# Two transformer blocks on one core: twelve more tiles by seven products, a convolution moved beside them, and a modulation taken in steps

## The chip, the cores and the metric

One core of one Trainium2 chip. The metric is the device time of one execution in microseconds; the kernel before has a median of 2616.32 us over 3 runs (2611.67 to 2616.39). The profile is of a run of its own, which took 2621.87 us.

## What is computed

Two blocks over 1024 tokens of width 1024, all in float32. The first block has a modulated norm, an SSM branch with a GLU, an attention over selected keys, a merge and an FFN. The second block, on which most of the change falls, projects its normed input `h` to gates and branch inputs and has three branches:

```python
gate_pre, a_in, a_z, b_uv, b_z, q, k, v, c_z, f_pre = split_columns(h @ w_in)

mod = cond @ w_mod + b_mod                       # first block: shift, scale, gate
u = rms_norm(h, norm1_g) * (1 + scale1) + shift1

# second block, branch a (conformer): a convolution of 31 taps over the tokens
a = a_in[..., :512] * sigmoid(a_in[..., 512:])
a = causal_depthwise_conv(a, conv_w, conv_b)
y_a = (silu(layernorm(a)) * silu(a_z)) @ w_a
# branch b (gmlp): v is mixed over the tokens of a chunk
y_b = (u * mixed(rmsnorm(v)) * silu(b_z)) @ w_b
# branch c (fox): attention with a forget gate
y_c = (attention(rmsnorm(q), rmsnorm(k), v, f_pre) * silu(c_z)) @ w_c
x = x + (g_a * y_a + g_b * y_b + g_c * y_c) @ w_out
```

## The kernel before

**Numbers.** Every float32 product on TensorE is made of three, each operand split in a high and a low part (`mm3`): high by high, high by low, low by high. ScalarE casts the high part (`wh`, L130), VectorE or GpSimd subtracts it for the low part (`wl`, L122). So a tile of 128 output columns over all tokens and a depth of 1024 takes 8 depth steps x 2 halves of 512 tokens x 3 products = 48 matmuls in `linear`. `linear_t` gives token-major output: 48 matmuls of 256 columns for a pair of token tiles.

**Seven products.** `wino` computes a pair of 128-column tiles by Strassen's scheme in Winograd's form: both the pair of tiles and the two halves of the tokens are cut in two along the depth too, and 7 products of quarter size take the place of 8. `wino_weights` makes sums of weights (`s<-wq`, GpSimd) and splits them (`vh`, `vl`). A pair costs 7 products x 4 depth steps x 3 = 84 matmuls of 512 columns where `linear` takes 96; in exchange the products must be added up: they are held as `snap` and reach the eviction function either whole or as a part to which a second one (`more`) is added.

**Order.** The program is recorded as one list for each engine by a scheduler; the engines run their lists in order and wait for each other by semaphores. The code steers the order with generators: `aside` is advanced once after each tile of `linear` (L159 matmuls), and in `wino` by a rate (`together`), so that VectorE work is spread beside TensorE work. `self.pace` and `self.tick` tie loads and other instructions to a matmul so that they are not put earlier.

**Stages that the change touches, in the order of TensorE:**

- The start, 0 to 80 us: transposes of `norm1`, then the first modulation. `mod_fast(part, half)` makes 512 values of scale or shift: 8 matmuls `p<-wmod` of one row by 256 columns (the other 256 columns are summed by VectorE into `macc`), a copy of the row to `macc` by ScalarE, 4 `turn` matmuls that turn it to a column, and an addition. `rest(half)` makes scale, scales 4 pages `xnt` on ScalarE, makes shift, and writes the split input `uh`, `ul` for half of the depth. The first two tiles of `proj1` come as 48 matmuls over the first half of the depth, then `between()`, which is all of `rest(1)`, then 48 over the second half.
- `glu`, about 490 to 583 us: 16 tiles of 24 matmuls `pl<-yh,wh`, with the key selection of the first attention (`topk`) on VectorE beside them as `aside`; GpSimd makes `wl` here. The `aside` step that ends `topk` runs straight on into `attend`, whose first act is a unit of logits (`pl<-akh,aqq`, then an exponent with a sum at L1182).
- `conv_in` 1541 to 1628 us; `plain_gates` to 1715 us: 8 tiles of `linear` for `a_z` (columns 4096, to DRAM page `az`) and `c_z` (columns 7680, to `fd`).
- `gates2` 1715 to 1943 us: 12 pairs by seven products, with `conv(0)` and `conv(1)` beside them, all of whose 31 taps are VectorE instructions of 512 tokens into PSUM (`p<-ca,small,p`).
- `fox` 1943 to 2124 us: q, k and v by `linear_t`, each tile with its norm (`xsl`), and a return through DRAM as `xraw`, scaled by GpSimd and transposed by TensorE. Beside it `conformer` runs `conv(2)` and `conv(3)` with every second tap on ScalarE (`ct`) and GpSimd (`cy<-cy,ct`), then the layer norm: a sum of squares `sqa` reduced by TensorE, a small chain on VectorE, and `diag` matrices by ScalarE from which TensorE spreads the factors; twice, for the mean and for the variance.
- `gmlp` 2124 to 2210 us: v by `linear_t`, then for each of 4 groups one tile of `b_z`, one of `b_u` by `linear`, and the mixing matmuls `p<-wst,gv`, whose result VectorE multiplies with both.

Of the kernel before, what the change touches and what calls it, by code (L numbers as in the profile page):

```python
# [12 lines left out]
AF = mybir.ActivationFunctionType  # L13
OP = mybir.AluOpType
# [3 lines left out]
T = 1024  # L18
# [50 lines left out]
class Core:  # L69
# [118 lines left out]
    def linear(self, w, cols, kt, xh, xl, evict, r0=0, half=None, between=None):  # L188
# [287 lines left out]
    def mod_fast(self, part, half):  # L476

        p = self.p1()
        acc = self.pg("macc2", bufs=2)
        for k in range(0, 8, 2):  # L480
# [4 lines left out]
            for j in range(2):  # L485
                c = self.cond[:, k + j:k + j + 1]
                self.mm(p[0:1, :256], c, w[:, j, 0:256], k + j == 0, k + j == 7)
# [4 lines left out]
        self.act(acc[0:1, 0:256], p[0:1, :256])  # L492
        p = self.p1()
        for j in range(4):
            n = 1 if j < 2 else 128
            self.mm(p[:, j:j + 1], acc[:n, j * 128:(j + 1) * 128], self.ones[:n, 0:1])
        m = self.small([4])
        c0 = part * 8 + half * 4
        self.tt(m, p[:, 0:4], self.v["b_mod"][:, c0:c0 + 4], OP.add)
        return m  # L500
# [40 lines left out]
    def norm1(self):  # L541
# [22 lines left out]
        def rest(half):  # L564

            ks = range(4 * half, 4 * half + 4)
            gs = self.small([4])
            self.stt(gs, self.mod_fast(1, half), 1.0, self.v["norm1_g"][:, 4 * half:4 * half + 4], OP.add, OP.mult)
            for k in ks:
                self.act(xnt[:, k], xnt[:, k], scale=gs[:, k % 4:k % 4 + 1])  # L570
            shift = self.mod_fast(0, half)
            self.wmark = self.last_mod
# [9 lines left out]
        rest(0)  # L582
        return uh, ul, lambda: rest(1)
# [1018 lines left out]
    def keep_x2(self):  # L1602
# [3 lines left out]
        for k in range(8):  # L1606
            x = self.pg("h", bufs=8)
            self.load(x, self.hd2[k], self.pace)
            self.ts(x, x, fg[:, k:k + 1])
            o = blocks(self.pg("xc", bufs=2))  # L1610
# [9 lines left out]
    def fox(self, hh, hl):  # L1620
# [74 lines left out]
        for j, (c0, gain) in enumerate(((6656, self.v["k_norm_g_2"]), (6144, gq))):  # L1695
            for g in range(2):
# [30 lines left out]
                start(unit_norm(g, j, gain, x, ss))  # L1727
        for g in range(2):
# [11 lines left out]
            self.linear_t(self.wraw(w, 0, 8, 7168 + 256 * g, 256), 8, hh, hl, ev_v)  # L1740

    def plain_gates(self, hh, hl, norm):
# [4 lines left out]
        def ev(dst, scale):  # L1747
            def f(m, p):
                z = self.pg("gst", bufs=2)
                self.mark = self.act(z, p, AF.Tanh, scale=0.5)  # L1750
                self.stt(z, z, 1.0, p, OP.add, OP.mult)
                if scale != 1.0:
                    self.act(z, z, scale=scale)
                self.load(dst(m), z)
# [11 lines left out]
    def gates2(self, x4, first):  # L1766

# [3 lines left out]
        for pair in range(12):  # L1771
# [11 lines left out]
            jobs.append((lambda pair=pair: self.wino_weights(w, 256 * pair), ev))  # L1783
        self.wino(jobs, x4, first)
# [113 lines left out]
    def gmlp(self, hh, hl):  # L1898
# [5 lines left out]
        for g in range(2):  # L1904
            def ev_v(i, p):
                x = v[i][:, :, 256 * g:256 * g + 256]
# [6 lines left out]
        def mix(t):  # L1913
            if t == 0:
                self.tt(ss[:, 0], ss[:, 0], ss[:, 1], OP.add)
                r = self.rsqrt_cols(ss[:, 0], 512)
                for i in range(8):
                    x = v[i // 2][:, i % 2]
                    self.act(x, x, scale=r[:, i:i + 1])
            yield  # L1920
            mx = self.pg("bb", bufs=4)
            for s in range(2):
                q = blocks(self.p1())
                for i in range(4):
                    self.mm(q[:, i], v[2 * s + i // 2][:, i % 2, t * 128:(t + 1) * 128], wst[:, t * 128:(t + 1) * 128])
                self.stt(blocks(mx[:, 512 * s:512 * s + 512]), q, self.v["gmlp_norm_g_2"][:, t:t + 1],
                         wst[:, None, 512 + 128 * t:640 + 128 * t].to_broadcast([128, 4, 128]), OP.mult, OP.add)
            self.bb.append(mx)
            yield
        steps = (None for t in range(4) for _ in mix(t))  # L1930
        self.hold = []

        def ev_z(m, p):
            th = self.pg("gz", bufs=2)
            self.act(th, p, AF.Tanh, scale=0.5)
            self.stt(th, th, 1.0, p, OP.add, OP.mult)
            self.hold.append(th)
            next(steps)

        def ev_u(m, p):  # L1940
            th = self.hold.pop(0)
            self.tt(th, th, p, OP.mult)
            next(steps)
            t = len(self.bb) - 1
            self.tt(self.bb[t], self.bb[t], th, OP.mult)
            self.show(f"bb{t}", self.bb[t])
        for t in range(4):
            self.linear(w, [(5632 + 128 * t, 128)], 8, hh, hl, ev_z)
            self.linear(w, [(4608 + 128 * t, 128)], 8, hh, hl, ev_u)

    def conv_in(self, hh, hl, norm):
# [3 lines left out]
        self.cyd = self.dram([2, 128, T], "cyd")  # L1955
# [24 lines left out]
    def conv(self, t, both):  # L1980


        gp, cw = self.nc.gpsimd, self.cw
# [3 lines left out]
        taps = range(30, -1, -2 if both else -1)  # L1987
        odd = list(range(29, -1, -2)) if both else []
        if both:
            y2 = self.pg("cy", bufs=2)  # L1990
            self.later(gp.memset(y2[:, 0:1], 0.0), self.pace)
        for h in range(2):
            acc = self.p1()
            c0 = 512 * h
            for n, k in enumerate(taps):
# [7 lines left out]
                if n % 2 == 1 and odd:  # L2003
                    for k2 in odd[:2]:
                        s, wk = 30 - k2, cw[:, k2, t:t + 1]
                        if s == 1:
                            i = self.act(y2[:, 1:], at[:, :T - 1], scale=wk)
                        else:
                            z = self.pg("ct", bufs=2)
                            i = self.act(z[:, s:], at[:, :T - s], scale=wk)  # L2010
                            self.tt(y2[:, s:], y2[:, s:], z[:, s:], OP.add, gp)
                        self.later(i, self.pace)
                    odd = odd[2:]
                if n % (4 if both else 8) == (3 if both else 7) and n < len(taps) - 1:
                    yield
            if h == 0 or not both:
                self.act(y[:, c0:c0 + 512], acc)
            else:
                self.tt(y[:, 512:], acc, y2[:, 512:], OP.add)
# [186 lines left out]
```

## Time and profile before

| | |
|---|---|
| median of 3 runs | 2616.32 us |
| profiled run | 2621.87 us, span 2620.2 us |
| mean granted TensorE clock | 0.984 |
| TensorE matmuls busy | 2515.9 us (96%) |
| VectorE / ScalarE / GpSimd busy | 63% / 43% / 32% |
| TensorE instructions of matmul | 12849 |

The profiled run is longer than the shown runs' median by 5.6 us. A busy time of TensorE counts overlapping rows once: a matmul of 512 columns has a row of 0.39 us, and the next one starts 0.23 us after it, so 96% says that TensorE was hardly ever without a matmul, not how fast each went. In 2620.2 us there are 104 us in which TensorE was idle.

### The profile page before, as it was taken

The page shows a single profiled execution, that of the slowest core. Times are in us where ns is not written, and L with a number is a line of the kernel's source. Part 1 is how long each engine was busy: PE and PEld are TensorE (multiplying, and loading weights), DVE is VectorE, ACT ScalarE, POOL GpSimd, SP SyncE. Part 2 cuts the span into 40 slices and gives each one's busy share as a digit, 9 for nine tenths or more (in the row PEclk, how much of TensorE's full clock was granted, in tenths as well). Part 3 has the DMA queues.
Part 4 walks back from the last instruction along what each step waited for, and adds up shares of the span by engine and source line. Part 5 has one row for each costly group of instructions (what it writes and reads, how often), then busy time and mean ns, then how long its engine had stood idle before and what let it go on. Part 6 is the DMA issues. An engine that isn't in the chain of part 4 may idle for free. (4 is left out here: it accounts for less than half of the span.)

```text
span 2620.2 us, 35143 instructions
## 1 busy us (share of the span) xinstructions
PE 2515.9 (96%) x12849; PEld 2119.9 (81%) x12849; DVE 1653.9 (63%) x2882; ACT 1129.7 (43%) x2144; POOL 847.9 (32%) x889
## 2 busy tenths in 40 slices
PE   6998999979999999999999999999999999999999
PEld 4877887768878788888888878888889997887887
DVE  6844889868894844444553367248768737548861
ACT  5323686828834433333322244234345433108830
POOL 2698441456500024444200120022318710005500
PEclk9999999989999999999999999999999999999999
DMA  7544453555294322222632244233362522586442
GB/s 256 158 152 139 143 167 112 192 168 132 73 332 154 124 90 89 70 91 81 223 135 85 87 131 149 85 105 121 113 206 77 166 77 73 183 235 156 135 159 83
DMA packets 272188, 360.37 MB, mean 138 GB/s; under 512 B 43948, under 2 KB 210552, under 8 KB 272016
## 3 DMA queue, kind: packets, MB, share of 16 engines
q1 hardware_dynamic: 270640, 356.89, 42.5%
q0 software_dynamic: 1152, 1.21, 0.3%
q8 instruction: 101, 1.65, 0.3%
q14 instruction: 71, 0.58, 0.1%
q10 hardware_dynamic: 224, 0.03, 0.0%
HBM read 262.65 MB, written 93.32 MB: 136 GB/s over the span
## 5 line engine op out<-in xcount | busy, mean ns | idle before, releaser
L130 ACT CAST wh<-wr 128x512 fp32r<-128x512 f32 (+1 forms) x308 | 170.7, 594 | 325.1 <-PE pl L159 125.9
L159 PE MATMUL pl<-uh,wh 128*128 128x512 f32 x672 | 266.6, 397 | 1.1 <-ACT uh L132 1.1
L159 PE MATMUL pl<-uh,wl 128*128 128x512 f32 x672 | 264.6, 394 | 0.6 <-DVE wl L122 0.6
L159 PE MATMUL pl<-ul,wh 128*128 128x512 f32 x672 | 263.9, 393 | 0.0
L122 POOL TENSOR_TENSOR s<-wq 128x512 f32<-128x512 f32 x60 | 84.8, 1415 | 480.1 <-DMA wq<-in_w_in_dram 268.6
L122 DVE TENSOR_TENSOR wl<-wr,wh 128x512 fp32r<-128x512 f32 (+1 forms) x260 | 179.1, 719 | 66.4 <-ACT wh L130 55.2
L122 DVE TENSOR_TENSOR snap<-pw,snap 128x512 f32<-128x512 f32 x90 | 61.9, 690 | 206.2 <-PE pw L159 116.9
L159 PE MATMUL pw<-xtl,vh 128*128 128x512 f32 x480 | 186.7, 389 | 0.0
L159 PE MATMUL pw<-xth,vl 128*128 128x512 f32 x480 | 185.3, 389 | 0.0
L159 PE MATMUL pw<-xth,vh 128*128 128x512 f32 x480 | 185.3, 389 | 0.0
L119 POOL TENSOR_SCALAR L<-L,small 128x128 f32<-128x128 f32 (+7 forms) x128 | 95.2, 747 | 259.8 <-DVE small L1186 253.1
L122 POOL TENSOR_TENSOR sqa<-sqa,sqn 128x512 f32<-128x512 f32 (+1 forms) x19 | 31.8, 1686 | 388.5 <-ACT sqn L132 206.8
L159 PEld LDWEIGHTS pl<-uh,wl 128*128 128x128 f32 x672 | 127.8, 190 | 27.7 <-DVE wl L122 1.1
L159 PE MATMUL p<-wth,uh 128*128 128x256 f32 x512 | 146.6, 287 | 3.1 <-DVE xsl L125 3.1
L159 PEld LDWEIGHTS pl<-uh,wh 128*128 128x128 f32 x672 | 127.6, 190 | 26.9 <-ACT uh L132 1.2
L159 PEld LDWEIGHTS pl<-ul,wh 128*128 128x128 f32 x672 | 127.9, 190 | 26.2 <-DVE ul L125 0.5
L159 PE MATMUL p<-wtl,uh 128*128 128x256 f32 x512 | 145.4, 284 | 0.0
L159 PE MATMUL p<-wth,ul 128*128 128x256 f32 x512 | 145.4, 284 | 0.0
L130 ACT COPY snap<-pw 128x512 f32<-128x512 f32 x90 | 52.6, 587 | 207.5 <-PE pw L159 196.6
L159 PE MATMUL pw<-uh,vh 128*128 128x512 f32 x360 | 140.0, 389 | 0.0
L159 PE MATMUL pw<-ul,vh 128*128 128x512 f32 x360 | 140.0, 389 | 0.0
L159 PE MATMUL pw<-uh,vl 128*128 128x512 f32 x360 | 136.6, 389 | 0.0
(448 smaller groups left out, 7264.0 us busy)
## 6 DMA issues: line engine op xcount, KB each, us to landing
wr<-in_w_in_dram SPq DMA_DIRECT2D x64, 512.0 KB, 4.8
wmod<-in_w_mod_dram SPq DMA_DIRECT2D x48, 512.0 KB, 6.3
wr<-in_w_out_dram SPq DMA_DIRECT2D x24, 512.0 KB, 6.2
wq<-in_w_in_dram SPq DMA_DIRECT2D x24, 512.0 KB, 5.2
gtd<-gst SPq DMA_DIRECT2D x24, 512.0 KB, 3.1
g_th<-gtd SPq DMA_DIRECT2D x24, 512.0 KB, 5.8
fd<-f_th SPq DMA_DIRECT2D x22, 512.0 KB, 3.4
f_th<-fd SPq DMA_DIRECT2D x22, 512.0 KB, 5.1
```

The source lines that it names most:

```text
L119: return (eng or self.nc.vector).tensor_scalar(out=out, in0=a, scalar1=s1, scalar2=s2, op0=op0, **kw)
L122: return (eng or self.nc.vector).tensor_tensor(out=out, in0=a, in1=b, op=op)
L130: return self.nc.scalar.copy(out, a)
L159: self.tick = self.nc.tensor.matmul(out, a, b, start=start, stop=stop, skip_group_check=True)
```

## The change

Four edits. **(1)** `c_z`, `b_z` and `b_u`, four tiles each, leave `plain_gates` and `gmlp` and become six more pairs of `gates2`. Their eviction functions read partial sums from SBUF and PSUM; the results of `b_z` x `b_u` go to DRAM (`bf`) and come back later. `gmlp` keeps v and a generator `mix` that `fox` advances. **(2)** `conv(2)` moves beside `gates2`, and `conv(3)`, alone beside `fox`, has all taps on VectorE; GpSimd and ScalarE have no taps any more. **(3)** The second half of the first modulation is advanced after each group of 12 matmuls; its row is copied by VectorE instead of ScalarE, and two of four scalings move to VectorE. **(4)** A `yield` stands between `topk` and `attend`.

```diff
@@ linear
                             for k in ks:
                                 self.mm3(p[:, h], wh[:, k], wl[:, k], xh[h][k], xl[h][k], k == 0, k == kt - 1)
-                    if ks[0] == 0:
-                        between()
+                            next(between, None)
@@ mod_fast
-        self.act(acc[0:1, 0:256], p[0:1, :256])
...
+        self.nc.vector.tensor_copy(acc[0:1, 0:256], p[0:1, :256])
+        def turn():
...
+        return turn
@@ rest
+            turn = self.mod_fast(1, half, half)
+            yield
             gs = self.small([4])
...
+            turn = self.mod_fast(0, half, half)
             for k in ks:
-                self.act(xnt[:, k], xnt[:, k], scale=gs[:, k % 4:k % 4 + 1])
+                g = gs[:, k % 4:k % 4 + 1]
+                if k % 4 < 2:
+                    self.act(xnt[:, k], xnt[:, k], scale=g)
+                else:
+                    self.ts(xnt[:, k], xnt[:, k], g)
+            yield
+            shift = turn()
@@ plain_gates
-        self.linear(w, [(4096 + 128 * t, 128) for t in range(4)], 8, hh, hl, ev(lambda m: self.az[m], 1.0))
-        self.linear(w, [(7680 + 128 * t, 128) for t in range(2)], 8, hh, hl, ev(lambda m: self.fd[m, 3, 0], 0.5))
+        self.linear(w, [(4096 + 128 * t, 128) for t in range(2)], 8, hh, hl, ev(0))
         first = self.wino_weights(w, 0, ref=self.tick)
-        self.linear(w, [(7680 + 128 * t, 128) for t in range(2, 4)], 8, hh, hl, ev(lambda m: self.fd[m + 2, 3, 0], 0.5))
+        self.linear(w, [(4096 + 128 * t, 128) for t in range(2, 4)], 8, hh, hl, ev(2))
@@ gates2
+        self.bf = self.dram([4, 128, T], "bf")
+        def silu(t, p, more):
+            if more is None:
+                more = p
+            else:
+                self.tt(more, p, more, OP.add)
+            self.mark = self.act(t, more, AF.Tanh, scale=0.5)
+            self.stt(t, t, 1.0, more, OP.add, OP.mult)
...
+            def ev_u(m, s, p, more, g=g, pair=pair):
+                t = g[m][:, 512 * s:512 * s + 512]
+                if more is None:
+                    self.tt(t, t, p, OP.mult)
+                else:
+                    self.tt(more, p, more, OP.add)
+                    self.tt(t, t, more, OP.mult, self.nc.gpsimd)
...
+            jobs.append((lambda pair=pair: self.wino_weights(w, 5632 + 256 * pair), ev_z))
+            jobs.append((lambda pair=pair: self.wino_weights(w, 4608 + 256 * pair), ev_u))
...
+            jobs.append((lambda pair=pair: self.wino_weights(w, 7680 + 256 * pair), ev_c))
@@ gmlp: the tiles of b_z and b_u go, mix() loads their product
-        for t in range(4):
-            self.linear(w, [(5632 + 128 * t, 128)], 8, hh, hl, ev_z)
-            self.linear(w, [(4608 + 128 * t, 128)], 8, hh, hl, ev_u)
+                f = self.pg("gz", bufs=2)
+                self.load(f, self.bf[t], self.pace)
...
+                self.tt(mx, mx, f, OP.mult)
@@ conv
-            taps = range(30, -1, -2 if both else -1)
...
-                            i = self.act(z[:, s:], at[:, :T - s], scale=wk)
-                            self.tt(y2[:, s:], y2[:, s:], z[:, s:], OP.add, gp)
+            for n, k in enumerate(range(30, -1, -1)):
@@ run
             self.topk(self.sc)
+            yield
             yield from self.attend(self.heads1)
...
-        self.aside = self.together(((None for t in range(2) for _ in self.conv(t, False)), 0.75))
+        self.aside = self.together(((None for t in range(3) for _ in self.conv(t, False)), 0.7))
...
         self.fox(hh, hl)
-        self.gmlp(hh, hl)
```

**TensorE at the start, before.** `p_330` are the turn matmuls of the first half's shift, `p_436` the first 8 matmuls of the second half's scale, `pl<-uh,wh` the first of the 48 matmuls over the first half of the depth.

```order
12 L159 MATMUL p_330<-small_63,macc_304 128x1 x4
13 L167 MATMUL p_363<-small_63 128x44
14 L159 MATMUL p_436<-wmod,small_63 1x256 x8
15 L159 MATMUL pl<-uh,wh 128x512 x2
16 L159 MATMUL pl<-ul,wh 128x512
```

The same place in the changed kernel; 23 matmuls of the linear stand between `p_400` and its turn `p_439`.

```order
14 L502 MATMUL p_330<-small_63,macc_300 128x1 x4
15 L167 MATMUL p_363<-small_63 128x44
16 L159 MATMUL pl<-uh,wh 128x512 x2
...
36 L159 MATMUL pl<-uh,wl 128x512
37 L487 MATMUL p_400<-wmod,small_63 1x256 x8
38 L159 MATMUL pl<-uh,wh 128x512
...
61 L502 MATMUL p_439<-small_63,macc_401 128x1 x4
62 L487 MATMUL p_446<-wmod,small_63 1x256 x8
63 L159 MATMUL pl<-uh,wh 128x512
64 L159 MATMUL pl<-ul,wh 128x512
65 L159 MATMUL pl<-uh,wl 128x512
66 L502 MATMUL p_489<-small_63,macc_447 128x1 x4
```

The second half's scale moved from ahead of the first linear matmul to behind 22 of them, its shift behind 45, and the last turn stands behind all 48.

**TensorE late in `glu`, before.** `pl<-yh,wh` are tiles of `glu`, `pl<-akh,aqq` the first logits of the attention; the two transposes of `small` are the last of `topk`'s on this engine.

```order
1963 L167 MATMUL p_5045<-small_63,small_4270 128x124
1964 L159 MATMUL pl<-yh,wl 128x512
...
2009 L159 MATMUL pl<-yh,wl 128x512
2010 L159 MATMUL pl<-akh,aqq 128x256
2011 L159 MATMUL pl<-akl,aqq 128x256
2012 L159 MATMUL pl<-yh,wh 128x512
```

In the changed kernel, from the same transpose on:

```order
1969 L167 MATMUL p_5037<-small_63,small_4270 128x124
1970 L159 MATMUL pl<-yh,wl 128x512
...
2110 L159 MATMUL pl<-yh,wl 128x512
2111 L159 MATMUL pl<-akh,aqq 128x256
2112 L159 MATMUL pl<-akl,aqq 128x256
```

Before, 46 matmuls of `glu` stand between that transpose and the logits, and four tiles behind them; now all 142 stand ahead of the logits.

**GpSimd as `fox` begins, before.** `cy<-cy,ct` are taps of the convolution, `wtl` the low parts of the weights of q, k and v.

```order
607 L1886 AFFINE_SELECT diag<-diag 128x512
608 L122 TENSOR_TENSOR cy<-cy,ct 128x1021
609 L122 TENSOR_TENSOR cy<-cy,ct 128x1019
610 L122 TENSOR_TENSOR wtl<-wr,wth 128x1024
611 L122 TENSOR_TENSOR cy<-cy,ct 128x1017
612 L122 TENSOR_TENSOR wtl<-wr,wth 128x1024
```

After:

```order
635 L1956 AFFINE_SELECT diag<-diag 128x512
636 L122 TENSOR_TENSOR wtl<-wr,wth 128x1024 x2
637 L122 TENSOR_TENSOR xraw<-xraw,small_16711 128x1024 x2
638 L122 TENSOR_TENSOR wtl<-wr,wth 128x1024
639 L122 TENSOR_TENSOR sqa<-cx 128x1024
640 L122 TENSOR_TENSOR xraw<-xraw,small_16711 128x1024 x2
```

All 28 rows `cy<-cy,ct` are gone from GpSimd; the scaling of `xraw` stands right behind the weights.

## Rows read from the trace of the kernel before

**Rows 1.** The page's busy times: engine, busy us, share of the span, instructions.
```profile
PE 2515.9 (96%) x12849; PEld 2119.9 (81%) x12849; DVE 1653.9 (63%) x2882; ACT 1129.7 (43%) x2144; POOL 847.9 (32%) x889
```
**Rows 2.** Stretches: start:end, us, PE, PEld, DVE, ACT, POOL busy, PEclk, DMA share, GB/s.
```profile
1800.00:1900.00 100.00, 100.00 (x443) 82.84 (x442) 73.98 (x97) 40.12 (x62) 29.61 (x21) 1.00 0.35 116
1943.00:2124.00 181.00, 171.20 (x1383) 168.96 (x1382) 128.00 (x192) 87.12 (x122) 110.45 (x49) 0.98 0.48 156
2023.00:2063.00 40.00, 40.00 (x339) 40.00 (x338) 28.50 (x45) 18.69 (x27) 21.83 (x11) 1.00 0.42 138
```
**Rows 3.** The page's costliest groups, a matmul of 512 columns: xcount, busy, mean ns.
```profile
L159 PE MATMUL pl<-uh,wh 128*128 128x512 f32 x672 | 266.6, 397 | 1.1 <-ACT uh L132 1.1
```
**Rows 4.** Timeline of PE at the start: start, us, instruction, count, [idle before <-releaser].
```profile
37.12 1.95 PE L159 MATMUL p<-small,macc 1*128 1x1 f32 x8 [4.76 <-ACT macc L130]
...
39.27 6.38 PE L159 MATMUL p<-wmod,small 128*1 128x256 f32 x16
45.57 0.72 PE L159 MATMUL pl<-uh,wh 128*128 128x512 f32 x2
...
57.72 3.62 PE L159 MATMUL p<-wmod,small 128*1 128x256 f32 x16
62.79 1.14 PE L159 MATMUL p<-small,macc 1*128 1x1 f32 x8 [1.45 <-ACT macc L130]
64.99 0.93 PE L159 MATMUL pl<-uh,wh 128*128 128x512 f32 x2 [1.07 <-ACT uh L132]
```
**Rows 5.** Timeline of ACT at the start.
```profile
32.56 4.27 ACT L132 ACTIVATE xnt<-xnt,small 128x1024 f32<-128x1024 f32 x4
36.72 0.34 ACT L130 COPY macc<-p 1x256 f32<-1x256 f32 x1
...
39.87 5.01 ACT L132 ACTIVATE uh<-xnt,small 128x512 fp32r<-128x512 f32 x8 [1.77 <-DVE small L122]
```
**Rows 6.** Timeline of PE in `glu`.
```profile
549.07 0.38 PE L159 MATMUL pl<-akh,aqq 128*128 128x256 f32 x1 [3.30 <-POOL aqq L122]
...
558.34 0.80 PE L159 MATMUL pl<-yh,wh 128*128 128x512 f32 x1 [8.77 <-DVE small L1182]
```
**Rows 7.** Timeline of POOL in `glu`.
```profile
552.20 2.52 POOL L122 TENSOR_TENSOR wl<-wr,wh 128x512 fp32r<-128x512 f32 x1
```
**Rows 8.** Groups of DVE instructions, 1743 to 1943 us (10.5 of the 12 pairs).
```profile
L125 DVE SCALAR_TENSOR_TENSOR p<-ca,small,p 128x512 f32<-128x512 f32 x60 | 45.1, 752 | 1.2
L122 DVE TENSOR_TENSOR vl<-s,vh 128x1024 fp32r<-128x1024 f32 x20 | 29.7, 1486 | 2.6 <-ACT vh L130 2.5
L122 DVE TENSOR_TENSOR snap<-pw,snap 128x512 f32<-128x512 f32 x31 | 21.3, 690 | 32.9 <-PE pw L159 16.5 <-ACT snap L130 16.1
L122 DVE TENSOR_TENSOR vl<-wq,vh 128x512 fp32r<-128x512 f32 x31 | 20.5, 685 | 1.3 <-ACT vh L130 1.3
```
**Rows 9.** Timeline of DVE: one operation beside GpSimd's sums and without them.
```profile
1696.84 3.03 DVE L122 TENSOR_TENSOR vl<-wq,vh 128x512 fp32r<-128x512 f32 x2 [6.83 <-ACT vh L130]
...
1726.47 1.29 DVE L122 TENSOR_TENSOR vl<-wq,vh 128x512 fp32r<-128x512 f32 x2
```
**Rows 10.** Timeline of PE in `fox` and `gmlp`: every idle time that it shows there.
```profile
1985.48 1.04 PE L167 MATMUL pl<-small,small 128*8 128x128 f32 x8 [1.36 <-DVE small L125]
...
2002.36 0.39 PE L159 MATMUL p<-wth,uh 128*128 128x256 f32 x1 [3.14 <-DVE xsl L125]
...
2075.14 1.11 PE L167 MATMUL p<-small,xraw 128*128 128x128 f32 x4 [5.30 <-POOL xraw L122]
...
2168.13 1.95 PE L159 MATMUL p<-small,sqa 128*128 128x1 f32 x16 [0.80 <-POOL sqa L122]
...
2180.43 0.66 PE L167 MATMUL pl<-small,diag 128*128 128x128 f32 x4 [4.08 <-ACT diag L130]
```
**Rows 11.** Groups of POOL instructions, 1943 to 2130 us, all lengths of one operation together.
```profile
L122 POOL TENSOR_TENSOR cy<-cy,ct 128x1021 f32<-128x1021 f32 (+13 forms) x28 | 72.7, 2598 | 7.3 <-ACT ct L132 5.9
...
L122 POOL TENSOR_TENSOR xraw<-xraw,small 128x1024 f32<-128x1024 f32 x8 | 15.1, 1904 | 15.2 <-DVE small L125 13.4 <-issue 1.8
```

More of the change, by code (lines that the diff above doesn't have):

```diff
@@ L486, in mod_fast @@
                 c = self.cond[:, k + j:k + j + 1]
-                self.mm(p[0:1, :256], c, w[:, j, 0:256], k + j == 0, k + j == 7)
+                i = self.nc.tensor.matmul(p[0:1, :256], c, w[:, j, 0:256], start=k + j == 0, stop=k + j == 7,
+                                          skip_group_check=True)
+                if ref is not None:
+                    self.later(i, ref)
                 if k + j == 0:
@@ L491, in mod_fast @@
                     self.stt(acc[:, 256:512], w[:, j, 256:], c, acc[:, 256:512], OP.mult, OP.add)
-        self.act(acc[0:1, 0:256], p[0:1, :256])
[L493 to L500, printed above, removed]
+        self.nc.vector.tensor_copy(acc[0:1, 0:256], p[0:1, :256])
+        def turn():
+            p = self.p1()
+            ref = self.tick if after else None
+            for j in range(4):
+                n = 1 if j < 2 else 128
+                i = self.nc.tensor.matmul(p[:, j:j + 1], acc[:n, j * 128:(j + 1) * 128], self.ones[:n, 0:1],
+                                          start=True, stop=True, skip_group_check=True)
+                if ref is not None:
+                    self.later(i, ref)
+            m = self.small([4])
+            c0 = part * 8 + half * 4
+            self.tt(m, p[:, 0:4], self.v["b_mod"][:, c0:c0 + 4], OP.add)
+            return m
+        return turn
     def mod_steps(self, parts):
@@ L1605, in keep_x2, with fetch @@
         self.x2 = self.dram([T, D], "x2")
-        for k in range(8):
+        ahead = []
+        def fetch(k):
             x = self.pg("h", bufs=8)
@@ L1609, in keep_x2 @@
             self.ts(x, x, fg[:, k:k + 1])
+            ahead.append(x)
+        fetch(0)
+        yield
+        for k in range(8):
+            x = ahead.pop(0)
+            if k < 7:
+                fetch(k + 1)
             o = blocks(self.pg("xc", bufs=2))
@@ L1727, in fox @@
                 start(unit_norm(g, j, gain, x, ss))
+        start(self.gmlp(hh, hl, advance))
         for g in range(2):
@@ L1930, in gmlp @@
[L1930 to L1946, printed above, removed]
@@ L1978, in conv_in, with conv @@
             part(2, s)
-    def conv(self, t, both):
-        gp, cw = self.nc.gpsimd, self.cw
+    def conv(self, t, keep):
+        cw = self.cw
         at = self.pg("ca", bufs=4)
@@ L2002, in conv @@
                 self.later(i, self.pace)
[L2003 to L2009, printed above, removed]
-                            i = self.act(z[:, s:], at[:, :T - s], scale=wk)
-                            self.tt(y2[:, s:], y2[:, s:], z[:, s:], OP.add, gp)
-                        self.later(i, self.pace)
-                    odd = odd[2:]
-                if n % (4 if both else 8) == (3 if both else 7) and n < len(taps) - 1:
-                    yield
[L2016 to L2019, printed above, removed]
-                self.tt(y[:, :512], y[:, :512], y2[:, :512], OP.add)
+                if n % 8 == 7:
+                    yield
+            self.act(y[:, c0:c0 + 512], acc)
             if h == 1:
                 self.show(f"conv{t}", y)
-                if both:
+                if keep:
                     self.cx[t] = y
@@ L2031, in conformer @@
         gp = self.nc.gpsimd
-        yield from self.conv(2, True)
         x = self.cx
-        for t in range(2):
-            x[t] = self.pg("cx", bufs=4)
-            self.load(x[t], self.cyd[t], self.pace)
-        yield from self.conv(3, True)
-        total = self.pg("sqa", bufs=4)
-        self.tt(total, x[0], x[1], OP.add, gp)
-        yield
-        self.tt(total, total, x[2], OP.add, gp)
+        for n, _ in enumerate(self.conv(3, True)):
+            if n == 3:
+                for t in range(3):
+                    x[t] = self.pg("cx", bufs=4)
+                    self.load(x[t], self.cyd[t], self.pace)
+                total = self.pg("sqa", bufs=4)
+                for y in (x[0], total):
+                    self.later(self.tt(total, y, x[1] if y is x[0] else x[2], OP.add, gp), self.pace)
+            yield
         self.tt(total, total, x[3], OP.add)
```

89 lines of the change are left out of this document (54 added, 35 removed).

## The prediction

> **What bounds the kernel now.** I read the busy times first [rows 1]: TensorE has a matmul in it for 2515.9 of 2620.2 us, so 104 us of idle time is all that waits can give back; any larger gain must take matmuls away. The stretches come second [rows 2]. Beside the pairs by seven products TensorE is busy for 100.00 of 100 us at full clock while VectorE is at 74%: there only the number of matmuls counts. 443 of them in 100 us are one every 0.226 us, and this pitch, not the 0.397 us of a row [rows 3], prices a matmul, since the rows overlap. In `fox` TensorE is idle for 10 of 181 us and GpSimd is busy for 110; where nothing waits, 339 matmuls of 256 columns take 40 us, 0.118 us each. The timelines then name each wait: at the start TensorE waits 4.76 us for a copy of one row [rows 4], late in `glu` 3.30 and 8.77 us [rows 6], in `fox` and `gmlp` five times, 14.7 us in all [rows 10].
>
> **Part 1, seven products.** Six pairs at 96 matmuls become six at 84: 72 fewer, x 0.226 = **-16.3 us**. (By the rows' 0.397 it would be 28.6, which a TensorE that is never idle can't give.) This needs VectorE to keep up. Of the last five to six jobs the order gives 62 taps, 13 `vl` of 512, 9 `vl` of 1024, 17 `snap` and 18 operations on `gst`; by [rows 8] that is 62 x 0.752 + 13 x 0.685 + 9 x 1.486 + 35 x 0.690 = 93 us, with two low parts of the next stage's weights some 95. Three `snap` to a job make this 5.7 jobs, and 5.7 x 84 x 0.226 = 108 us. So VectorE goes from 74% to 88%, with 13 us of slack. ScalarE (40%) and GpSimd (30%) have room for the tanh and the eviction products. Stalls of single evictions are not in the trace of before, since its TensorE never waits there; they cost between 0 (the slack holds) and 9 us (the lock, below). I take **+2**, near the low end, because the sum stays under 108. The four stores and four loads of `bf`, 512 KB each, come where the DMA engines are at 35 to 48% [rows 2]; the loads are issued a stretch ahead and I cost them at nothing. If that cover failed, the mixing product of VectorE would be late, behind which nothing of TensorE stands until branch b.
>
> **The lock, weighed.** Two `vl` took 3.03 us where GpSimd was making its sums, and 1.29 us a little later [rows 9], 0.87 us more for each. Yet 31 of them have a mean of 0.685 [rows 8] against 0.645 for the free one: with GpSimd busy for 30% of the time, hardly any met it. By the mean, my +2 stands. The Trainium skill, page "SBUF — State Buffer", section "Who interferes with whom", speaks against the change here: a VectorE instruction with two SBUF inputs and a GpSimd instruction that reads SBUF take turns on a shared port, and the second to issue blocks for the whole instruction. The trace agrees in the one place of [rows 9]; what it would make of the sum is rival B.
>
> **Part 2, the start.** Before, the row of the shift is copied by ScalarE behind four scalings of 4.27 us [rows 5], and the turn waits until 37.12 [rows 4]. Now VectorE copies it; TensorE was done 4.76 us before 37.12, at 32.36, and I allow 1.3 us for the low parts then on VectorE (the price of the free pair in [rows 9]) plus the copy: 33.7, that is 3.4 us earlier. The input `uh` follows the turn, as before. `p_436`, 16 passes of 6.38 us at the lower clock (3.62 us for as many later, [rows 4]), no longer stands ahead of the first linear matmul, but is moved, not removed; TensorE now stands idle between the end of the turn at 35.7 and the first `uh` and `ul`, some 1.7 us (0.8 us from turn to `uh` before [rows 4, 5], then one `uh` of 0.6 and the start of one `ul`). The two waits of the second half, 1.45 and 1.07 us [rows 4], go, since 20 and more matmuls stand beside each step. 3.4 + 1.45 + 1.07 - 1.7 = 4.2, and with the slow matmuls that follow the second idle time (0.93 us for two, [rows 4]) I take **-5 us**. Bounds: -2.5 (only the two waits) to -9 (also the 2.8 us between the two prices of 16 passes).
>
> **Part 3, the `yield`.** The logits leave the middle of `glu`. The 3.30 us for `aqq` and the 8.77 us for the exponent's unit at L1182 [rows 6] no longer hold a tile of `glu`. What is late next is GpSimd's `wl` for that tile, 552.20 + 2.52 = 554.72 [rows 7]; TensorE restarted at 558.34, so **-3.6 us**. Bounds: 0 (another of the tile's inputs came as late) to -12.1 (both waits whole).
>
> **Part 4, `fox`.** 28 additions on GpSimd, 72.7 us, go [rows 11]; `xraw`, whose 15.1 us on GpSimd had a wait of 5.30 us behind them, then has the engine nearly to itself. VectorE keeps its load: 64 taps before (16 even taps, two halves, two convolutions), 62 after. So the 5.30 goes, half of the 3.14 for `xsl` (1.6), and the 0.80 and 4.08 of `gmlp` [rows 10], whose layer norm now stands in `fox`: 11.8 us. Put back: the chain from a sum of squares to `diag` took from 2170.08 to 2180.43, 10.35 us [rows 10]; the order now puts 100, 96 and 57 matmuls at 0.118 us between its steps, 11.8, 11.3 and 6.7 us, so the last step is late by 3.6, and 0.4 is put down for the others. Net **-7.8 us**. Bounds: -14.7 (all five waits go) to +6 (each of three steps of the norm late by its 3.6, and two waits like the 5.30 and 3.14 come back, against the 11.8 saved).
>
> **Sum.** -16.3 + 2 - 5 - 3.6 - 7.8 = -30.7 us: the profiled run of 2621.87 becomes 2591. That run is 5.6 us above the median of the runs shown; against 2616.3 the forecast is **2586 us**. A change under 0.2%, 5 us, is about what a measurement of this kernel can't tell from none.
>
> **Rivals.**
> - **A: only the count pays.** What the waits give back is met by the next wait: the start ends at the weights or at GpSimd, `fox` at its norm. For it: three engines release the five waits [rows 10], so where one is early another may be the last. Against: the largest of them, 5.30 us, hangs on GpSimd, whose additions are plainly gone. -16.3 + 2 = 2602 us.
> - **B: VectorE becomes the bound beside the six new pairs**, by the lock. The 22 `vl` and 2 `gst` with both inputs in SBUF, at 0.87 us more each, make 95 into 116 us, 8 to 9 over the 108; the time is 2586 - 2 + 9 = 2593. It decides only if more than 15 of the 24 meet GpSimd. Against it stands the mean of 0.685. The Trainium skill, page "Perfetto Trace Analysis", section "Optimizing Scalar/DVE Operations", would have work taken off a saturated VectorE to ScalarE or even GpSimd; the change goes the other way with its taps, so that page speaks for this rival.
> - **C: slower.** VectorE's 62 taps in `fox`, now of one convolution and in one row, stand ahead of the `xsl` of each token tile in VectorE's queue; TensorE needs what `xsl` yields for 16 transposes. If each waits 3.14 us, as one does before [rows 10], that is 50 us in place of 3. From 11 on, this takes back all of the 31 us; with all 16 the time is 2586 + 47 = 2633. Against it: the number of taps is what it was, and 15 of 16 waited for nothing.
> - That the change doesn't do what it says is no case: the order shows 72 fewer matmuls, the moved logits and no `cy`.
>
> **Chances.** Forecast 0.58 (its own range 2577 to 2594), A 0.20, B 0.14, C 0.04, no measurable change because of several of these at once 0.04. Forecast, A and B are all faster by over 5 us: faster 0.92, same 0.04, slower 0.04. The range reaches down to 2568 (start -9, `glu` and `fox` at half of what lies beyond my values, -4 and -3.5, no stalls) and up to A with its stalls, 2603.
>
> **What would show it.** In the profile after: 72 fewer rows of 512 columns on TensorE; TensorE still idle for nothing, or a few us, beside the six new pairs, VectorE near 88%; the first linear matmul near 37.5 instead of 45.57, and no waits near 63 and 65; no wait of TensorE for L1182 among tiles of `glu`, but one for `wl`; no wait for `xraw`, one of some 3 us for `diag` in `fox`. Wrong it would be if waits for `snap` or `gst` stood in the six jobs with VectorE over 95% (B), if TensorE waited for `xsl` at most tiles of `fox` (C), or if the idle sum stayed at 104 us (A).

## The result, and the profile after

| | before | after |
|---|---|---|
| median | 2616.36 us (2611.67 to 2617.57, 4 runs) | 2577.24 us (2575.64 to 2580.30, 4 runs) |
| ratio, 95% interval | | 0.9859 (0.9847 to 0.9871) |
| profiled run | 2621.87, span 2620.2 | span 2574.3 |

The change saves 39 us by the medians (34 to 40 by the interval of the ratio), where 31 were forecast. The profiled spans differ by 45.9 us; some 4 us of that belong to the one execution that the profile of before shows, whose stretch from the attention's projection to the FFN (712 to 948 us) is 2.5 to 4.3 us longer than that of any later profile, the kernel with the start alone changed included. Some 4.5 us more lie in its second block, as shown below.

The page's busy times after, to be held against [rows 1]: 72 matmuls fewer, VectorE up by 43 us, TensorE idle for 84 us instead of 104.

```profile
PE 2490.6 (97%) x12777; PEld 2102.3 (82%) x12777; DVE 1697.2 (66%) x2976; ACT 1114.5 (43%) x2144; POOL 822.0 (32%) x889
```

Stretches of the changed kernel: `plain_gates`, the pairs by seven products in thirds (the last is the six new ones), and two that hold `fox` and what follows. The columns are those of [rows 2].

```profile
1624.00:1668.00 44.00, 44.00 (x196) 36.44 (x195) 15.95 (x15) 8.19 (x11) 9.92 (x7) 1.00 0.28 96
1668.00:1778.00 110.00, 110.00 (x487) 91.06 (x486) 75.23 (x97) 44.17 (x68) 30.65 (x23) 1.00 0.35 115
1778.00:1890.00 112.00, 112.00 (x496) 92.74 (x495) 86.87 (x112) 48.15 (x74) 33.96 (x24) 1.00 0.33 112
1890.00:2002.00 112.00, 112.00 (x496) 92.74 (x495) 93.13 (x123) 42.59 (x68) 41.30 (x28) 1.00 0.32 100
2002.00:2130.00 128.00, 124.92 (x1013) 122.85 (x1012) 98.21 (x185) 50.40 (x85) 34.79 (x17) 1.00 0.47 161
2130.00:2254.00 124.00, 124.00 (x939) 118.69 (x938) 82.87 (x112) 44.76 (x80) 9.63 (x4) 1.00 0.60 192
```

Beside the new pairs VectorE is busy for 93 of 112 us, 83% (forecast: 88%), and TensorE for all of it. From 1624 us to the end of branch a, all its waits are these two (waits: TensorE's instruction, its releaser, us in total, times, longest), against the five of [rows 10]:

```profile
PE p L167 <- POOL xraw L122: 1.6, 1, 1.6
PE pl L159 <- DVE wtl L122: 1.5, 1, 1.5
```

The granted clock stays at 1.00 there. Before, three stretches of 10 us had less:

```profile
2070.00:2080.00 10.00, 4.86 (x26) 4.86 (x27) 7.66 (x17) 4.83 (x7) 7.68 (x5) 0.66 0.50 155
2165.00:2175.00 10.00, 8.95 (x49) 7.62 (x48) 5.83 (x17) 6.07 (x11) 2.38 (x1) 0.83 0.23 52
2175.00:2185.00 10.00, 5.92 (x28) 4.87 (x27) 4.66 (x11) 2.02 (x3) 0.00 (x0) 0.83 0.16 52
```

That is 10 x (0.34 + 0.17 + 0.17) = 6.8 us of full clock. In part of it TensorE stood idle, and that part is counted as a wait already:

```profile
2070.00:2075.00 5.00, 0.00 (x0) 0.00 (x0) 4.76 (x12) 1.62 (x3) 2.75 (x2) 0.74 0.31 116
```

Counted by slices of 1 us, each by the share in which TensorE was busy, 5.4 us are left. The last matmul of branch a lies at 2358.3 us before and 2313.1 after, the first of `plain_gates` at 1633.1 and 1624.1: this piece is shorter by 36.2 us. 16.3 of count, 15.5 - 3.1 = 12.4 of idle time (the waits of [rows 10] and two small ones for `att`, 0.8 us) and 5.4 of clock make 34.1.

How much of this is one execution? The kernel with the start alone changed has the code of before in the second block; its four engines run the same instructions in the same order past the wait for `xraw`, and TensorE to the end of branch a. In its profile the piece takes 720.6 us, not 725.1. All its waits there make 9.9 us instead of 15.5, 6.1 us go to the clock, and the wait for `xraw` is short:

```profile
2067.55 0.66 PE L167 MATMUL p<-small,xraw 128*128 128x128 f32 x4 [0.55 <-POOL xraw L122]
```

Against that profile the changed kernel's piece is 31.6 us shorter. Two profiles give 32 to 36 us, and the largest wait of [rows 10], 5.30 us, doesn't repeat.

The start, timeline of TensorE (one row from VectorE), against [rows 4]:

```profile
32.64 0.41 DVE L495 COPY macc<-p 1x256 f32<-1x256 f32 x1 [0.20 <-PE p L487]
```
```profile
36.52 0.73 PE L159 MATMUL pl<-uh,wh 128*128 128x512 f32 x2 [2.09 <-ACT uh L132]
37.95 0.80 PE L159 MATMUL pl<-ul,wh 128*128 128x512 f32 x1 [0.70 <-DVE ul L125]
...
44.31 3.62 PE L487 MATMUL p<-wmod,small 128*1 128x256 f32 x16
...
58.80 1.14 PE L502 MATMUL p<-small,macc 1*128 1x1 f32 x8
61.01 0.73 PE L159 MATMUL pl<-uh,wh 128*128 128x512 f32 x2 [1.07 <-ACT uh L132]
```

The linear begins 9 us earlier, its second half 4.0 us earlier, and all of it ends 3.8 us earlier (74.06 against 77.83). Then the two kernels meet at `kin`, pages that GpSimd scales for the index of the attention. First the row of before, then that of after:

```profile
125.83 0.66 PE L167 MATMUL p<-small,kin 128*128 128x128 f32 x4 [1.89 <-POOL kin L122]
```
```profile
126.71 1.11 PE L167 MATMUL p<-small,kin 128*128 128x128 f32 x4 [5.86 <-POOL kin L122]
```

The gain of the start is there as 4 us more of waiting, and the matmuls after it run at the lower clock (0.50 from 125 to 135 us, where before had 0.59); at 146 us both kernels are level (145.8).

In `glu`, the exponent's 8.77 and the 3.30 of [rows 6] are gone, and one wait takes their place. TensorE, then GpSimd's queue ahead of the `wl` that it waits for:

```profile
553.29 0.79 PE L159 MATMUL pl<-yh,wl 128*128 128x512 f32 x1 [8.54 <-POOL wl L122]
```
```profile
542.45 2.40 POOL L122 TENSOR_TENSOR g_th<-g_tg,g_th 128x1024 f32<-128x1024 f32 x1 [7.00 <-DVE small L425]
544.92 2.61 POOL L122 TENSOR_TENSOR aqq<-aq,aqq 64x1024 fp32r<-64x1024 f32 x1
547.61 3.13 POOL L119 TENSOR_SCALAR g_tg<-g_tg 128x1024 f32<-128x1024 f32 x1
550.72 2.52 POOL L122 TENSOR_TENSOR wl<-wr,wh 128x512 fp32r<-128x512 f32 x1
```

### The profile page after: what moved, and what is told of

Its sections match the earlier page's. It is cut to its first block, busy times and chain, and to the rows that moved or that the text cites. A ratio compares the mean times of both kernels' runs of the same rounds, so it can differ in the third digit from the quotient of the medians.

```text
span 2574.3 us, 35098 instructions
## 1 busy us (share of the span) xinstructions
PE 2490.6 (97%) x12777; PEld 2102.3 (82%) x12777; DVE 1697.2 (66%) x2976; ACT 1114.5 (43%) x2144; POOL 822.0 (32%) x889
## 5 line engine op out<-in xcount | busy, mean ns | idle before, releaser
L159 PE MATMUL pw<-xtl,vh 128*128 128x512 f32 x576 | 224.1, 389 | 0.0
L159 PE MATMUL pw<-xth,vh 128*128 128x512 f32 x576 | 222.8, 389 | 0.0
L159 PE MATMUL pw<-xth,vl 128*128 128x512 f32 x576 | 222.3, 389 | 0.0
L122 DVE TENSOR_TENSOR wl<-wr,wh 128x512 fp32r<-128x512 f32 x236 | 160.2, 708 | 59.1 <-ACT wh L130 51.4
L159 PE MATMUL pl<-uh,wh 128*128 128x512 f32 x480 | 191.0, 399 | 3.2 <-ACT uh L132 3.2
L159 PE MATMUL pl<-ul,wh 128*128 128x512 f32 x480 | 189.7, 395 | 0.8 <-DVE ul L125 0.7
L159 PE MATMUL pl<-uh,wl 128*128 128x512 f32 x480 | 190.0, 396 | 0.0
L125 DVE SCALAR_TENSOR_TENSOR p<-ca,small,p 128x512 f32<-128x512 f32 (+9 forms) x240 | 177.9, 743 | 4.1
L159 PEld LDWEIGHTS pw<-xtl,vh 128*128 128x128 f32 x576 | 108.1, 188 | 22.5
L159 PEld LDWEIGHTS pw<-xth,vl 128*128 128x128 f32 x576 | 108.1, 188 | 22.4
```

The lines of the kernel that those rows point to most:

```text
L122: return (eng or self.nc.vector).tensor_tensor(out=out, in0=a, in1=b, op=op)
L125: return self.nc.vector.scalar_tensor_tensor(out=out, in0=a, scalar=s, in1=b, op0=op0, op1=op1)
L159: self.tick = self.nc.tensor.matmul(out, a, b, start=start, stop=stop, skip_group_check=True)
```

## The experiments

| kernel | median us | ratio to before, 95% interval |
|---|---|---|
| the change | 2577.24 | 0.9859 (0.9847 to 0.9871) |
| the change again | 2576.41 | 0.9850 (0.9835 to 0.9865) |
| without the `yield` | 2580.46 | 0.9856 (0.9838 to 0.9873) |
| with the old start | 2580.62 | 0.9855 (0.9836 to 0.9873) |
| before, with the new start alone | 2612.39 | 0.9989 (0.9980 to 0.9998) |
| tiles back by 8 products | 2593.26 | 0.9910 (0.9893 to 0.9927) |
| convolution back in `fox`, taps on GpSimd | 2607.58 | 0.9967 (0.9955 to 0.9979) |
| additions on GpSimd in `fox` | 2601.31 | 0.9947 (0.9932 to 0.9962) |
| memsets on GpSimd in `fox` | 2589.26 | 0.9900 (0.9886 to 0.9915) |
| `kin` on VectorE | 2579.82 | 0.9862 (0.9845 to 0.9878) |
| `tg` on ScalarE | 2569.67 | 0.9826 (0.9805 to 0.9846) |
| `tg` on ScalarE, `aqq` on VectorE | 2571.40 | 0.9835 (0.9821 to 0.9848) |

Each ratio is to runs of the kernel before taken along with that row, whose medians are 2614.4 to 2616.4 us. Most intervals reach 3 to 5 us to either side, so 3 us between two medians of this table are not told from none: by the ratios, the rows without the `yield` and with the old start are as fast as the change.

The kernel of the change, run again beside others, gave this:

> The changed kernel once more, on the chip of the two runs beside it, to see what repeats: the time within 0.2% of 2577 us; kin near 126.7 us, wl's wait of 8.5 us in glu, and no wait over 2 us from the six pairs to the end of fox should repeat. The start of the FFN's pairs (939 us) tells how far the first block varies between executions of one program.

It gave 2576.41 us, the waits for `kin` (5.8 us) and `wl` (8.6 us) again, and no wait over 2 us in `fox`. The FFN's pairs began at 940.6 us, against 939.2; the two kernels with additions and memsets, which differ from it only later, have this point at 943.3 and 943.6. Differences of 4 us between single profiles of the first block say little.

**The tiles: does VectorE keep up?** One part undone, with three convolutions beside twelve pairs:

```diff
-        self.linear(w, [(4096 + 128 * t, 128) for t in range(2)], 8, hh, hl, ev(0))
+        self.linear(w, [(4096 + 128 * t, 128) for t in range(4)], 8, hh, hl, ev(lambda m: self.az[m], 1.0))
+        self.linear(w, [(7680 + 128 * t, 128) for t in range(2)], 8, hh, hl, ev(lambda m: self.fd[m, 3, 0], 0.5))
...
+        self.gmlp(hh, hl)
```

> The changed kernel with the twelve tiles back by 8 products in plain_gates and gmlp; three convolutions now beside the twelve old pairs, VectorE there at 85 + 139 = 225 of 228 us, 99%. Theory: the count alone, 72 x 0.226 = 16.3 us slower, and up to 3 us of waits for VectorE, and 0 to 5 us for the layer norm's steps between other tiles: 2593 to 2601 us. Rival B (VectorE as the bound, with the lock against GpSimd): from 99% on every us more is a wait; with 30 of 60 vl at 0.87 us more it is 26 us beyond that, 2620 us or more.

16.0 us slower than the change, where the count says 16.3; the two agree better than the intervals could promise, and in the profiles the piece from `plain_gates` to the end of branch a is 14.7 us longer. A stretch of its twelve pairs:

```profile
1750.00:1850.00 100.00, 100.00 (x443) 82.82 (x442) 94.74 (x126) 42.29 (x65) 30.28 (x23) 1.00 0.35 116
```

VectorE at 95%, GpSimd at 30%, and TensorE waits for nothing. Rival B is refuted here at a higher load than it was made for. The kernel also shows what the convolution's move is worth while `gmlp` still has its tiles: from `plain_gates` to the end of branch a it is 21.5 us shorter than before, 17.0 shorter than the kernel with the start alone, and its TensorE waits there are 0.6 and 0.5 us.

**The convolution.** The other part undone, the new pairs kept:

```diff
-        self.aside = self.together(((None for t in range(3) for _ in self.conv(t, False)), 0.7))
+        self.aside = self.together(((None for t in range(2) for _ in self.conv(t, False)), 0.5))
...
+        yield from self.conv(2, True)
+        yield from self.conv(3, True)
```

> The changed kernel with the convolution as before: conv(2) and conv(3) beside fox, odd taps on ScalarE and GpSimd; the six pairs stay. Theory (GpSimd's additions are what TensorE waited for in fox): waits for xraw, xsl and small values come back, some 10 us, and with them stretches at the lower clock, 3 to 7 us: 2587 to 2594 us, and the small integer operations on VectorE (128x32) take 0.9 us again. Rival (the gain in fox comes from the layer norm and the tiles that left gmlp): 0 to 3 us slower, 2577 to 2580 us.

30 us slower, more than either theory had (2607.58, at most 2594 expected). TensorE's waits from 1624 us to the end of branch a:

```profile
PE p L159 <- POOL sqa L122: 6.2, 1, 6.2
PE p L159 <- DVE xsl L125: 3.8, 1, 3.8
PE pl L167 <- ACT diag L130: 3.1, 1, 3.1
PE pl L167 <- DVE small L125: 2.6, 1, 2.6
PE pl L159 <- DVE wl L122: 2.4, 1, 2.4
PE p L167 <- POOL xraw L122: 1.7, 1, 1.7
```

These are 19.8 us, 16.7 more than in the changed kernel, and 6.5 us more go to the clock while TensorE is busy: together nearly the 24 us by which the piece is longer. 6 more come after it, in the second attention. Without the moved convolution the tiles bring little: this kernel is 8.7 us faster than before, with the start and the `yield` in it, and 4.8 faster than the kernel with the start alone, with the `yield` in it. By the profiles, from `plain_gates` to the end, it is 0.8 us shorter than the one with the start alone and 6.8 shorter than the one of before, where 72 matmuls fewer are worth 16.3. That the eight tiles which leave `gmlp` were the cover under which GpSimd's additions and the layer norm ran fits this: the longest of these waits, 6.2 us for `sqa`, was 0.80 us before, when a tile of `gmlp` stood right ahead of it. No run changes the cover alone.

**What of GpSimd holds `fox` up?** 28 additions whose result nobody reads, on GpSimd alone; then 84 memsets in their place.

```diff
...
+                if keep and n % 2 == 1 and n < 29:
+                    self.later(self.tt(y2[:, 12:], y2[:, 12:], at[:, :1012], OP.add, self.nc.gpsimd), self.pace)
```

> The changed kernel with 28 additions of 128x1012 put on GpSimd beside conv(3) in fox, whose result nobody reads; VectorE and ScalarE have the same instructions as in the changed kernel. Theory (GpSimd's additions held up fox, through the engine itself and through VectorE): VectorE's small operations slow down again (those on 128x32 integers from under 0.3 to about 0.9 us), waits for xraw and xsl of some 5 to 10 us come back with 3 to 7 us of lower clock, 2582 to 2592 us. Rival (only the taps' place on ScalarE and VectorE matters, and the place of the layer norm): under 2 us, 2577 to 2579 us.

```diff
...
+                    for j in range(3):
+                        self.later(self.nc.gpsimd.memset(y2[:, 180:], 0.0), self.pace)
```

> The same, with 84 memsets of 128x844 in place of the 28 additions: about as long on GpSimd (by the 0.53 us of a memset of 512 columns some 73 us), but they read nothing from SBUF. Theory (VectorE is held up by GpSimd's reads): the small operations stay under 0.3 us; only what waits in GpSimd's own queue (xraw behind a memset, at most some 3 us) remains: 2577 to 2582 us. Rival (GpSimd is merely busy, and xraw and the weights' low parts come late): as with the additions.

From the first matmul of `fox` to the last of branch a: 310.9 us in the change, 329.4 with the additions, 315.2 with the memsets, though GpSimd spends 70.9 us on the ones and 67.5 on the others. Groups of VectorE, 2002 to 2254 us, in the order: change, memsets, additions.

```profile
L122 DVE TENSOR_TENSOR wtl<-wr,wth 128x1024 fp32r<-128x1024 f32 x7 | 10.3, 1471 | 0.1
L125 DVE SCALAR_TENSOR_TENSOR small<-small 128x32 f32<-128x32 f32 x24 | 6.4, 268 | 0.4
...
L119 DVE TENSOR_SCALAR small<-small 128x32 int32<-128x32 int32 x8 | 1.3, 166 | 0.1
```
```profile
L122 DVE TENSOR_TENSOR wtl<-wr,wth 128x1024 fp32r<-128x1024 f32 x7 | 10.3, 1473 | 0.1
L125 DVE SCALAR_TENSOR_TENSOR small<-small 128x32 f32<-128x32 f32 x24 | 6.4, 265 | 0.3
L119 DVE TENSOR_SCALAR small<-small 128x32 int32<-128x32 int32 x8 | 4.3, 535 | 0.1
```
```profile
L122 DVE TENSOR_TENSOR wtl<-wr,wth 128x1024 fp32r<-128x1024 f32 x7 | 16.3, 2323 | 0.0
L125 DVE SCALAR_TENSOR_TENSOR small<-small 128x32 f32<-128x32 f32 x24 | 10.6, 442 | 0.3
L119 DVE TENSOR_SCALAR small<-small 128x32 int32<-128x32 int32 x8 | 10.0, 1254 | 0.1
```

Before, the integer operations took 1242 ns. In these rows instructions with two inputs are slower beside additions and as fast as in the change beside memsets; the integer operations with one input are slowed by both, by additions more. TensorE's largest waits in the stretch, with the additions:

```profile
PE p L167 <- POOL xraw L122: 9.1, 2, 8.4
PE pl L167 <- DVE small L125: 6.3, 1, 6.3
```

The wait of 8.4 us ends with GpSimd, but GpSimd's queue was not what held it: that engine had itself stood idle and waited for the small operations of VectorE.

```profile
2098.09 3.76 POOL L122 TENSOR_TENSOR xraw<-xraw,small 128x1024 f32<-128x1024 f32 x2 [3.71 <-DVE small L125]
```

So most of the loss comes through VectorE, and most of that needs additions: the stretch loses 18.4 us to additions and 4.3 to memsets of about the same length in total. An addition reads SBUF and takes 2.5 us where a memset takes 0.8; these runs don't part the two. The additions cost more than expected (24 us slower, 2582 to 2592 expected): 18 of it in `fox`, 4 before it and 3 after it. My expectation for the memsets was too good in its total as well (12 us slower, 2577 to 2582 expected): 4 of these lie in `fox`, 4 before it and 4 after it in the profile, the latter two where I did not look for a cause (behind it, one wait of TensorE of 3.3 us ends on nothing that the profile shows); and the small integer operations did not stay under 0.3 us.

By the Trainium skill, page "SBUF — State Buffer", section "Who interferes with whom", a VectorE instruction with two SBUF inputs contends with a GpSimd instruction that reads SBUF, not with one that only writes it; the rows of `wtl`, with two inputs, agree: 1471, 1473 and 2323 ns.

**The start.** Undone in the change, and alone on the kernel before:

```diff
-                            next(between, None)
+                    if ks[0] == 0:
+                        between()
...
```

> The changed kernel with the first modulation as before (all of the second half between the two halves of the matmuls, row copied by ScalarE). Theory of the forecast: the start's gain reaches the end, 3.8 to 5 us slower than the changed kernel, 2581 to 2582 us. Rival (the next wait, for kin on GpSimd near 126 us, takes the gain): 0 to 2.5 us slower, 2577 to 2580 us, with PE reaching the matmuls behind the norms of k (146 us) at the same time in both.

> The kernel before with the first modulation in steps and nothing else. Theory (GpSimd's kin near 126 us takes the start's gain): TensorE is through with both halves some 3.8 us earlier (near 74 us), waits for kin until 126 us as before, and the time is that of before, 0 to -2 us: 2613 to 2616 us. Rival (the forecast's -5 us reaches the end): 2611 us or less.

3.4 us slower without it by the medians, which the intervals don't tell from none (0.9855 against 0.9859); 3.9 faster with it alone (by the ratio 0.5 to 5.2). In the profile of the latter both halves are done near 75.1 us, and then:

```profile
127.78 1.12 PE L167 MATMUL p<-small,kin 128*128 128x128 f32 x4 [5.88 <-POOL kin L122]
```

So the theory of `kin` is right about 126 us; its conclusion, no gain in the end, is not borne out by the kernel with the start alone, and the other run can't decide. All profiles together say more than a single one. The first matmul of `glu` starts at 465.2 and 466.6 us in the two kernels with the old start, and between 460.7 and 464.4 us in the eleven with the new one, 2.7 us earlier on average, though two are few. At the index matmuls near 158 us nothing of this is seen yet; at the first matmul that reads `s_Q`, near 213 us, about half of it is. What gives it back stays open.

**Taking `kin` off GpSimd.**

```diff
-                            r[:, 8 + 4 * s:12 + 4 * s, None].to_broadcast([128, 4, 64]), OP.mult, nc.gpsimd)
+                            r[:, 8 + 4 * s:12 + 4 * s, None].to_broadcast([128, 4, 64]), OP.mult)
```

> The changed kernel with the four scalings of kin in proj1 on VectorE instead of GpSimd. Theory (TensorE's 5.9 us at 126.7 us are GpSimd's queue, which takes the start's gain): kin is ready near 123 instead of 126.6 us, the wait is 2 us and the lower clock behind it shorter; 3 to 6 us faster at the index matmuls (158 us), and 1 to 6 us at the end: 2571 to 2576 us. Rival (GpSimd's chain of the SSM parameters is what the stage ends on anyway): at 465 us the same as the changed kernel, 2577 us.

```profile
123.54 1.36 PE L167 MATMUL p<-small,kin 128*128 128x128 f32 x8 [2.15 <-DVE kin L122]
```

The transposes came 3.2 us earlier, the next ones (`kx`) 4.3, the index matmuls 2.4, and at 464 us nothing was left: 2579.8 us, no gain. The rival's time holds; that GpSimd's chain takes the gain is not shown.

**The `yield`, and the wait behind it.**

```diff
             self.topk(self.sc)
-            yield
             yield from self.attend(self.heads1)
```

> The changed kernel without the yield between the selection and the first logits. Theory (the yield saves a wait of its own): the waits for aqq (3.3 us) and for the exponent's unit (8.8 us) come back into glu and the 8.5 us for wl goes; from the two traces glu would be 3.6 us longer and the attention 1.8 us shorter, so 1.7 to 3.6 us slower than the changed kernel, 2579 to 2581 us. Rival (the attention, bound by VectorE, gives all of it back): no difference, 2577 us.

3.2 us slower by the medians, which the intervals don't tell from none (0.9856 against 0.9859); the waits of 3.3 and 8.8 us are back, as the theory says. In the profiles `glu` takes 117.2 us instead of 113.8, and the attention behind it, from the last matmul of `glu` to the first of its projection, 129.8 instead of 131.2: of 3.4 us in `glu` 2.0 stay.

```diff
-            self.ts(tg, tg, 1.0, None, OP.add, eng=self.nc.gpsimd)
+            self.act(tg, tg, bias=1.0)
```

> The changed kernel with the addition of 1 to tg in glu on ScalarE instead of GpSimd. Theory (the 8.5 us for wl in glu is GpSimd's queue of g_th 2.4, aqq 2.6, tg 3.1, wl 2.5 us): wl comes 3.1 us earlier, the wait is 5.4 us, and with the clock 3 to 5 us faster: 2572 to 2574 us. Rival (VectorE's selection or the next weights end that wait): 2577 us.

```profile
544.82 0.52 PE L159 MATMUL pl<-yh,wl 128*128 128x512 f32 x1 [4.16 <-POOL wl L122]
```

The wait halves, from 8.54 to 4.16 us; `glu`'s last matmul comes 7.5 us earlier, of which 1.6 were there when it began. With 2569.67 us it is the fastest kernel here, faster than theory and rival said; its interval ends where that of the change begins, and overlaps that of the change run again. With `aqq` off GpSimd as well (this edit stands on the one above):

```diff
-            self.tt(q[64:], x[64:], f32(q[64:]), OP.subtract, nc.gpsimd)
+            self.tt(q[64:], x[64:], f32(q[64:]), OP.subtract, nc.gpsimd if h else None)
```

> The changed kernel with the addition to tg in glu on ScalarE and the first head's aqq on VectorE, both off GpSimd. Theory (GpSimd's queue is what wl waits for): the 4.2 us that are left before wl go nearly whole, 2 to 4 us faster than with tg alone: 2565 to 2568 us. Rival (VectorE's selection, which aqq now delays, holds the second half of the tile): the same as with tg alone, 2570 us, or 1 to 2 us slower.

2571.40 us: no more to be had that way, as the rival says. The wait for `wl` is down to 0.9 us at most, and one of 3.5 us stands a little later; its cause isn't shown, so that it is the selection on VectorE stays open.

## Why the prediction was right, and where it was off

Right in direction and within its range, 8 us too small: 2577.24 lies at the very edge of the forecast's own 2577 to 2594. (The lower end of the whole range, 2568, isn't what the terms beside it make: 2586 - 4 - 4 - 3.5 - 2 is 2572.5.) By its parts:

- **Seven products**, -16.3 + 2: measured 16.0 by the medians (2593.26 against 2577.24), 14.7 by the profiles. The pitch of 0.226 us was the right price. The 2 us for stalls of evictions didn't come; one wait of 1.5 us for `wtl` stands at the seam to `fox`.
- **The start**, -5: 3.9 us by the medians of the kernel with it alone (0.5 to 5.2 by the ratio), not told from none in the other pair. The turn began at 33.11 us (worked out: 33.7), the first `uh` at 35.74 and the first linear matmul at 36.52 (37.5); the idle time behind the turn was 2.09 + 0.70 us (1.7); of the two waits of the second half that were to go only the 1.45 us went, the 1.07 us for `uh` stands at 61.01 us with the slow matmuls behind it. GpSimd's `kin` takes the gain at 126 us (rival A's way), but some of it is back at `glu`.
- **The `yield`**, -3.6: right for `glu` (3.4 us by the profiles), by the wait that the text named as the next, `wl`, ending at 553.29 us (worked out: 554.72). The attention's loss of 1.4 us was put at nothing; 2.0 us are left, too few for the medians to tell.
- **`fox`**, -7.8: this is the step that failed, a term sized at less than half of what it is. By the twin that has only the tiles undone the piece is 21.5 us shorter than before and 17.0 shorter than with the start alone. Of the 21.5, the 14.7 us of waits less 1.1 and the 5.4 us of clock, which I left uncounted, make 19.0. What I "put back" was wrong: the step from the sum of squares to `diag`, 10.35 us before, had VectorE's products of `gmlp` in its midst. In the changed kernel the reduction ends at 2141.09 us, `diag` is made from 2145.73 to 2146.87, 5.8 us later, and TensorE takes it at 2148.31 without a wait. And the half of `xsl`'s wait that I kept is gone; `xsl` itself takes 744 ns as before. That this is because the small operations ahead of it in VectorE's queue are faster without GpSimd's additions is argued, not shown.

The path to the largest wait, 5.30 us for `xraw`, was wrong too. I had `xraw` wait for GpSimd's additions; GpSimd had stood idle for 2.25 us and waited for VectorE, whose first three small operations of this chain took 5.04 us while GpSimd ran `wtl` and one of the additions:

```profile
2063.46 5.04 DVE L119 TENSOR_SCALAR small<-small 128x32 f32<-128x32 f32 x3
```
```profile
2073.18 3.76 POOL L122 TENSOR_TENSOR xraw<-xraw,small 128x1024 f32<-128x1024 f32 x2 [2.25 <-DVE small L125]
```

That the wait went (1.6 us are left) was right by way of VectorE, not of GpSimd's queue, and its size was that of one execution.

The undone parts cost 16.0, 30.3, 3.4 and 3.2 us, 53 in all, not 39: the first two are not independent. The tiles alone, with the old convolution, bring 1 to 7 us by the profiles, in place of 16. My parts priced each edit against the kernel before and could not see this. Rival A (2602) would have held had `fox` ended on its norm; rival C had no wait for `xsl` at all. Of the signs, VectorE's 83% beside the new pairs was near the 88%, the wait for `diag` didn't come, and 1.6 us for `xraw` stayed where none was forecast.

## What to carry to other kernels

When an edit takes matmuls from a stage, ask what else runs under them: here the tiles were worth 16 us with the convolution moved in the same change, and 1 to 7 without. Count the clock with each wait that goes, but only where the engine is busy: here 15.5 us of waits had 5.4 us of lower clock behind them, and 9.9 us had 6.1 in another profile of the same block. Follow a wait past its releaser: the engine that ends it may have been waiting itself. Price a step of a chain by its own instructions, not by a stretch in which other work stood in the same queue. And before a single wait is priced, see it in a second profile: the 5.30 us were 0.55 there.

## What the runs showed of the hardware that I had not expected

In the 252 us from the start of `fox` on, VectorE instructions on 128x32 integers with one input, whose own work is the same, took 166 ns on average in the change, 535 ns with 84 GpSimd memsets in the stretch and 1254 ns with 28 GpSimd additions; SCALAR_TENSOR_TENSOR on 128x32 floats took 268, 265 and 442 ns. And VectorE could be 95% busy, with GpSimd at 30%, beside pairs by seven products without one wait of TensorE in 100 us.
